# A planned instruction order for the second attention: other starting times, two early slab loads, 196 shifted ranks, and another order of the last down sweeps

## The chip, the cores and the metric

The kernel runs on one core of one Trainium2 chip. The metric is the device time of one execution in microseconds (us), as the median of several runs. The parts of the core that matter here are TensorE (PE, with its weight loads PEld), VectorE (DVE), ScalarE (ACT), GpSimd (POOL) and SyncE (SP), which issues the DMAs. Each engine works through its own instructions in the order in which they were issued to it; an instruction that waits holds up all that stands behind it on its engine.

## The reference, cut to what matters

Two layers over 1024 latent tokens and 256 context tokens, with 1024 features in fp32. Layer 0 mixes with a neighbourhood attention, layer 1 with a sliding-window attention; each layer ends with a gated feed-forward.

```python
for i in range(DEPTH):                                   # DEPTH = 2
    h  = modulate(rmsnorm(x, g_attn[i]), sh1, sc1)       # shift, scale, gate from SiLU(c)
    hc = modulate(rmsnorm(ctx, g_attn[i]), sh1c, sc1c)
    q, k, v = attn_inputs(h, w_in, gq, gk, n_kv)         # one projection, RMS norm of q and k per head
    ...                                                  # layer 1: rotary, then banded softmax with a
    o = sliding_window_attention(q, k, v, k_c, v_c, sink)  # sink logit, 16 heads in 4 key groups
    x = x + gt1 * (o @ w_out)
    h = modulate(rmsnorm(x, g_ffn[i]), sh2, sc2)
    x = x + gt2 * conv_ffn(h, w_up[i], conv_w[i], conv_b[i], w_down[i])
```

## The kernel before, in words

Every fp32 product is done as three matmuls on a high and a low part of each operand (`whi`, `wlo` of a weight; `h1hi`, `h1lo` or `n1lo` of the activations). Splitting a weight takes a DMA into a `raw` buffer (three of them), a copy on ACT (`whi`) and a subtraction on DVE or POOL (`wlo`).

The kernel is a row of stages: layer 0's attention, its feed-forward `ffn(0)`, layer 1's attention (here: the second attention), and `ffn(1)`. In each stage the work is written as operations with an engine, a planned duration, what they read and write, and a key. A planner (`Sched`) plays the stage through: at each moment every free engine takes the ready operation with the smallest key, if the buffers that it needs are free in the plan. The instructions are then issued in the order that came out, and that order is fixed. `Sched.rank` adds a number from a table (`RANKS`) to the keys of some operations, named by their index. The stage of the first attention has such a table (`na`), and both feed-forwards have one; the second attention has none.

`Sched.run(free)` takes the times at which the engines become free; the second attention calls it without, so that in the plan all engines are free at time 0, though on the chip the queues still hold the end of `ffn(0)`.

The second attention goes like this. `plan_ctx_kv` projects the context to keys and values (`mm<-whi,h1chi`, weights `ckv`), which have their own norm (`ckvv`, `ckvy`) and end in the tile `ckc`. `plan_norm` normalises the second half of the tokens: it needs the sums of squares (`sums`), loads that half back from DRAM (`x<-x_dram`, four tiles), and makes `t`, `h1hi` and `n1lo` from it. The first half is ready when the stage begins (`h1hi`, `h1lo`). For each of 4 key groups, four `slab` tiles of weights are loaded and split, eight token tiles are projected (`plan_sw_qkv`: `mm`, then `qraw`, `qsq`, `qv`, a power on POOL `qy`, the rotary `qa` and `qb`, and transposes `pt<-idr,st`), and sixteen units of softmax follow (`plan_sw_su`: scores `s`, maximum on DVE, a copy of the sink logit on POOL `S<-sink`, exponential on ACT `S<-S,m`, transposes `pt<-idr,S`, their split `pthi`, `ptlo`, and the products `pv`). The last group's units are mixed with the output projection of the first 512 tokens (`mm<-o0hi,whi`), for which stored heads are loaded back (`oraw`) with the reciprocals of their sums, multiplied and split (`o0hi`, `o0lo`, and `o1hi`, `o1lo` for the second 512).

The feed-forward ends with five sweeps over the down weights (`plan_pair`, matmuls `dn`), numbered 0 to 4. Sweep 2 fills the four banks `c`, whose results each go to one output tile; sweep 4 fills the four banks `d`, each of which goes to two. `plan_ev` adds a bank to its output tile on DVE (`xn<-dn,modc,xn`), `plan_xd` stores the tile.

Of the kernel before, what the change touches and what calls it, by code (L numbers as in the profile page):

```python
# [11 lines left out]
F32 = mybir.dt.float32  # L12
F32R = mybir.dt.float32r
AF = mybir.ActivationFunctionType
# [3 lines left out]
P = 128  # L18
# [20 lines left out]
class InOrder:  # L39
# [7 lines left out]
    def __getattr__(self, name):  # L47
        f = getattr(self.eng, name)

        def call(*a, **k):  # L50
# [31 lines left out]
          19.7},  # L82
    ffn1={286: 3.3, 290: 17.8, 2323: -3.8},
)


class Sched:
# [6 lines left out]
                                       pool=(0.15, 0.08, 0.06, 0.1), dma=(0.0, 0.0, 0.0, 0.0)).items()  # L94
# [164 lines left out]
def trunk_kernel(ctx, tc, xperm, xtok, xseq, cc, wmod0, wmod, bmod, gnorm, na_wqkv, na_gq, na_gk, na_bias, na_wo,  # L259
# [38 lines left out]
    dve.memset(invd, 1.0 / D)  # L298
    dsh = spool.tile([P, 112], F32, name="dsh")[:, :8]
    mhalf = cpool.tile([P, 16], F32, name="mhalf")  # L300
# [67 lines left out]
    def t_dve(n):  # L368
        return 0.065 + n / 960.0

    def t_act(n):
        return 0.094 + n / 1200.0
# [4 lines left out]
    def t_pool(n):  # L377
        return 0.15 + n / 480.0
# [59 lines left out]
    class Slabs:  # L438
# [29 lines left out]

        def plan(self, sc, i, key, uses):
            sc.op("dma", 1.4, lambda e: self.load(i), writes=[("raw", i)], key=key - 7, acq=[("raw", ("raw", i), 2)])  # L470
            sc.op("act", t_act(768), lambda e: self.hi(i), reads=[("raw", i)], writes=[("wh", i)], key=key - 2,
                  acq=[("w", ("w", i), uses)], rel=[("raw", i)])
            sc.op(*self.engs, lambda e: self.lo(i, e), reads=[("raw", i), ("wh", i)],
                  writes=[("wl", i)], key=key - 2, rel=[("raw", i)])

# [192 lines left out]
    def plan_norm(sc, l, psa, wk, sums, x, hl, key):  # L668
# [68 lines left out]
        for k in range(KT):  # L737
            hi = hl[0][:, k, :]

            def mul(e, k=k):  # L740
                B["t", k] = wk.tile([P, 512], F32, tag=("pthi", "ptlo")[k % 2], name="t", bufs=PTB)
                dve.scalar_tensor_tensor(out=B["t", k][:, :n], in0=x[:, k, :], scalar=modc[:, l, 0, 1, k:k + 1], in1=B[f[1]][:, :n],
                                         op0=ALU.mult, op1=ALU.mult)
            sc.op("dve", t_dve(n) + 0.06 * l, mul, reads=[f, ("x1", k)], writes=[K("t", k)], key=key, rel=[f],
                  acq=[(("pthi", "ptlo")[k % 2], K("t", k), 1)], port=l == 0)
# [21 lines left out]
            for k, lof in los[-2:]:  # L767
                sc.op(*(("pool", t_pool(n)) if l == 1 and k % 2 else ("dve", t_dve(n))), lof, reads=[K("hi", k), K("t", k // 2 * 2 + 1)], writes=[(f"h{l}", 1, k)], key=key, rel=[K("t", k)])

# [308 lines left out]
    NWAIT = (2, 3, 4)  # L1078
    NREADY = 8.0
    NPRE = 3  # L1080
# [277 lines left out]
    def ffn(l, opj, xt1, todo):  # L1358
# [694 lines left out]
        def plan_pair(si, i):  # L2053
# [60 lines left out]
            for q in range(nq):  # L2114
                d, starts = prods[q]
                for m in range(4):
                    def mm(e, q=q, m=m, d=d, starts=starts):
# [6 lines left out]
                    sc.op("pe", 3 * t5, mm, reads=[I + (t, q) for t in ("gh", "gl", "wh", "wl")] + u_done,  # L2124
                          writes=[("dn", d, m)], key=k0 + 2.72 * q + (1.36 * m - 2.72 * (i - NP + 2) if si == 4 and i >= NP - 2 else 0),
                          acq=[("b", ("d" + d, m), dict(a=3, b=2, c=1, d=2)[d])] if starts and i == 0 else (),
# [10 lines left out]
        def plan_xd(c, k, key):  # L2137
# [6 lines left out]
            sc.op("dma", 0.9, out_, reads=[("xn", c, k)], writes=[("xd", c, k)], key=key, rel=[("xnt", c, k // 2)])  # L2144
        for si in range(5):
            for i in range(NP):
                plan_pair(si, i)
            ke = KS[si + 1]
            if si == 0:
# [47 lines left out]
    def plan_next(sc, KS, xn, bank, x_tile, plan_sums, plan_bc, plan_t, plan_hilo, u_done, gp, D_):  # L2197
# [85 lines left out]
        for i in range(4):  # L2283
# [10 lines left out]
            def lo(e, i=i):  # L2294
# [9 lines left out]
    slabs = Slabs(sw_wqkv, WL1)  # L2304
    ffn(0, op0, None, [0, 1])
    gqk, sink, bandt, rc, rs = [C1[n] for n in ("gqk", "sink", "bandt", "rc", "rs")]
# [345 lines left out]
    h[1] = [hpool.tile([P, KT, 512], F32R, tag="hhi", name="h1hi", bufs=2), Parts([None] * 4, 2)]  # L2652
    sc.hold("raw", "sums1", 1)
    for i in range(4):
        sc.hold("w", ("cw", i), 2)
    for tag in ("s", "pt"):
        psa(tag, F32)
    plan_ctx_kv()
    for j in range(0, KT, 2):
        sc.op("dma", 1.2, lambda e, j=j: dma.dma_start(  # L2660
            xs[1].tiles[j // 2], x_dram[:, (KT + j) * 512:(KT + j + 2) * 512].rearrange("p (k t) -> p k t", k=2)),
            writes=[("x1", j), ("x1", j + 1)], key=-206)
# [50 lines left out]
    xt1 = plan_oproj1()  # L2713
    sc.run()
    ph.close()
# [118 lines left out]
```

## Time and profile before

| | us |
|---|---|
| median of 3 runs | 2786.18 |
| lowest, highest | 2782.22, 2786.51 |
| the profiled execution | 2783.58 |
| its span in the profile | 2781.8 |
| PE busy in the span | 2750.7 (99%) |
| DVE, ACT, POOL busy | 2260.3, 1693.5, 409.8 |

The span is the time from the first to the last instruction of the profiled execution. In the timeline of the profile a row gives its start, its duration, its engine, the operation with its output and inputs, and in brackets how long the engine had stood idle before it and what ended that wait. All operations pass through one helper, so that every row has the line L51; operations are told apart by the names of their tiles.

### The profile page before, as it was taken

How to read it: one execution, taken by the hardware profiler on the slowest of the kernel's cores; microseconds unless marked ns; L12 is line 12 of the kernel's file. 1: busy time of each engine (PE TensorE's matmuls, PEld its weight loads, DVE VectorE, ACT ScalarE, POOL GpSimd, SP SyncE). 2: the span in 40 equal slices, each digit the busy share in tenths (PEclk: the TensorE clock that was granted, in tenths of full speed). 3: DMA queues.
4: the chain of work that ended last, by engine and by line, in shares of the span. 5: the costliest groups of instructions: out<-in, count | busy, mean ns of one | idle time of the engine just before them, and what ended most of it. 6: DMA issues, size and time to landing. Idle time of an engine off the chain costs nothing.

```text
span 2781.8 us, 45781 instructions
## 1 busy us (share of the span) xinstructions
PE 2750.7 (99%) x16297; PEld 2439.2 (88%) x16297; DVE 2260.3 (81%) x4982; ACT 1693.5 (61%) x3320; POOL 409.8 (15%) x662
## 2 busy tenths in 40 slices
PE   8999999999999999999999999999999999999999
PEld 7999999999899987777788879999988888888887
DVE  6887888888789687877788688888886988888757
ACT  6776776788556544445454457888863655455443
POOL 1222222223100000000000007545430000000000
PEclk9999999999999999999999999999999999999999
DMA  7222222224745543444466561000255322324745
GB/s 284 81 83 91 71 73 73 90 80 132 253 152 189 184 163 133 163 148 144 152 222 235 170 223 39 24 24 20 72 187 179 104 107 98 114 105 144 256 151 189
DMA packets 144870, 375.63 MB, mean 135 GB/s; under 512 B 22144, under 2 KB 35072, under 8 KB 143232
## 3 DMA queue, kind: packets, MB, share of 16 engines
q1 hardware_dynamic: 144640, 372.70, 39.8%
q8 instruction: 128, 2.10, 0.3%
q14 instruction: 102, 0.84, 0.1%
HBM read 305.59 MB, written 67.04 MB: 134 GB/s over the span
## 4 chain that ended last, share of the span: by engine, by line
PE 95%; DVE 2%; DMA 1%; ACT 1%; issue 0%; POOL 0%; SPq 0%; DVEq 0%; ACTq 0%
PE mm L51 18%; PE ua L51 17%; PE dn L51 15%; PE uc L51 13%; PE pt L51 7%; PE pv L51 6%; PE s L51 5%; PE oacc L51 5%; PE ud L51 4%; PE dnc L51 2%; PE u L51 2%; PE mod L51 1%; DMA x<-in_xperm_dram 0%; DMA slab<-in_sw_wqkv_dram 0%; DVE S L51 0%
## 5 line engine op out<-in xcount | busy, mean ns | idle before, releaser
L51 ACT ACTIVATE whi<-wraw 128x512 fp32r<-128x512 f32 (+1 forms) x264 | 213.1, 808 | 200.5 <-PE uc L51 58.4
L51 DVE TENSOR_TENSOR wlo<-wraw,whi 128x512 fp32r<-128x512 f32 (+1 forms) x264 | 240.2, 911 | 41.4 <-ACT whi L51 41.0
L51 DVE TENSOR_TENSOR ptlo<-pt,pthi 128x512 fp32r<-128x512 f32 (+2 forms) x384 | 223.9, 596 | 34.9 <-ACT pthi L51 31.7
L51 ACT ACTIVATE S<-S,m 128x640 f32<-128x640 f32 (+3 forms) x288 | 221.0, 769 | 38.0 <-DVE m L51 29.6
L51 PE MATMUL dn<-ghi,whi 128*128 128x512 f32 x616 | 239.8, 389 | 0.0
L51 PE MATMUL dn<-ghi,wlo 128*128 128x512 f32 x616 | 239.7, 389 | 0.0
L51 PE MATMUL dn<-glo,whi 128*128 128x512 f32 x616 | 239.6, 389 | 0.0
L51 ACT ACTIVATE pthi<-pt 128x512 fp32r<-128x512 f32 (+2 forms) x384 | 196.3, 524 | 64.1 <-PE pt L51 48.8
L51 DVE SCALAR_TENSOR_TENSOR u<-c,cv,u 128x1023 f32<-128x1023 f32 x176 | 222.9, 1279 | 6.4 <-ACT u L51 5.4
L51 ACT ACTIVATE whi<-s 128x1024 fp32r<-128x1024 f32 (+1 forms) x116 | 109.0, 939 | 181.8 <-PE uc L51 129.3
L51 ACT ACTIVATE ghi<-graw 128x512 fp32r<-128x512 f32 x154 | 96.3, 630 | 177.5 <-PE dn L51 102.2
L51 PE MATMUL pt<-idr,S 128*128 128x128 f32 x1280 | 196.5, 274 | 3.2 <-DVE qt L51 2.2
L51 PE MATMUL mm<-whi,h0hi 128*128 128x384 f32 x480 | 172.2, 359 | 0.6 <-ACT qraw L51 0.6
L51 DVE TENSOR_TENSOR glo<-graw,ghi 128x512 fp32r<-128x512 f32 x154 | 105.3, 688 | 73.0 <-ACT ghi L51 67.1
L51 PE MATMUL mm<-wlo,h0hi 128*128 128x384 f32 x480 | 162.3, 338 | 0.0
L51 PEld LDWEIGHTS pt<-idr,S 128*128 128x128 f32 x1280 | 150.4, 141 | 10.7 <-ACT kkl L51 2.3
L51 DVE TENSOR_TENSOR wlo<-s,whi 128x1024 fp32r<-128x1024 f32 (+1 forms) x116 | 124.7, 1075 | 39.2 <-ACT whi L51 39.1
L51 POOL TENSOR_TENSOR qy<-qv,mhalf 128x4 f32<-128x4 f32 (+1 forms) x112 | 121.5, 1088 | 156.4 <-DVE qv L51 134.9
L51 POOL TENSOR_TENSOR n1y<-n1v,mhalf 128x4 f32<-128x4 f32 (+1 forms) x8 | 8.2, 1026 | 922.5 <-DVE n1v L51 922.5
L51 PEld LDWEIGHTS dn<-glo,whi 128*128 128x128 f32 x616 | 115.6, 188 | 24.1
L51 PEld LDWEIGHTS dn<-ghi,whi 128*128 128x128 f32 x616 | 115.6, 188 | 24.1
L51 PEld LDWEIGHTS dn<-ghi,wlo 128*128 128x128 f32 x616 | 115.6, 188 | 23.7
(386 smaller groups left out, 8828.0 us busy)
## 6 DMA issues: line engine op xcount, KB each, us to landing
wraw<-in_w_up_dram SPq DMA_DIRECT2D x132, 512.0 KB, 3.5
wm<-in_wmod_dram SPq DMA_DIRECT2D x80, 512.0 KB, 3.9
wraw<-in_w_down_dram SPq DMA_DIRECT2D x44, 512.0 KB, 4.1
graw<-g_dram SPq DMA_DIRECT2D x44, 512.0 KB, 4.4
wraw<-in_w_down_dram SPq DMA_DIRECT2D x88, 256.0 KB, 3.1
graw<-g_dram SPq DMA_DIRECT2D x66, 256.0 KB, 2.8
slab<-in_na_wqkv_dram SPq DMA_DIRECT2D x32, 384.0 KB, 3.9
woraw<-in_na_wo_dram SPq DMA_DIRECT2D x24, 512.0 KB, 4.2
```

Of the source, the lines that this page charges most:

```text
L51: r = f(*a, **k)
```

## The change

The second attention is planned with other numbers:

- its planner starts with ACT, DVE, POOL and SP busy for 5.5, 9.0, 0.5 and 9.0 us (`LAG`);
- operations without an instruction (`stored`) hold back the loads of the four `x` tiles in the plan until given times; the norm's tiles `n1lo` now wait in the plan for the release of the `x` tiles (`xl`); a `raw` buffer may be released out of order;
- a small ACT operation (`table`, on one column) stands early in the stage, so that the table of the exponential is loaded there;
- the loads of the first two `slab` tiles are issued by `plan_next`, at the end of `ffn(0)`, and the splits of the first group's slabs get a key of their own;
- 196 operations get a shift of their key (`RANKS["sw"]`); the norm's key goes from -260 to 5, and `NREADY` from 8.0 to 9.2 (a planned time of the first attention).

In `ffn(1)` the sweeps run in the order 0, 1, 3, 4, 2 in place of 0, 1, 2, 3, 4 (`ffn(0)` keeps its order).

```diff
+    sw={7: 5.7, 60: 47.4, 133: -7.4, 167: -41.6, 188: 22.2, 198: -62.9, 214: 25.5, 231: 15.5, 238: 3.4, 256: 1.9,
...
-    ffn1={286: 3.3, 290: 17.8, 2323: -3.8},
+    ffn1={286: 3.3, 290: 17.8, 2330: -3.8},
...
+    LAG = dict(act=5.5, dve=9.0, pool=0.5, dma=9.0)
+    STORED = {0: 2.0, 2: 7.5, 4: 3.0, 6: 10.0}
+
+    def table(sc, f, src, tok, key):
+
+        sc.op("act", 1.4, lambda e: act.activation(small[:, 64:65], src(), f, scale=0.0), reads=[tok], writes=[("table",)], key=key)
...
-    NREADY = 8.0
+    NREADY = 9.2
...
-        KS = [KD, KD + 60, KD + 120, KD + 150, KD + 180, KD + 210]
+        SWEEPS = (0, 1, 3, 4, 2) if last else (0, 1, 2, 3, 4)
+        KS = {si: KD + (0, 60, 120, 150, 180)[q] for q, si in enumerate(SWEEPS)}
...
+        for i in range(NSLAB):
+            sc.op("dma", 1.4, lambda e, i=i: slabs.load(i), reads=[("slr", 3), ("sll", i)], writes=[("slab", i)], key=KS[5] - 30,
+                  acq=[("raw", ("slab", i), 1)])
...
-    sc = Sched(dict(CAPS, qraw=3))
+    sc = Sched(dict(CAPS, qraw=3, xl=4), {"raw"})
...
     plan_ctx_kv()
+    table(sc, AF.Exp, lambda: CK["v", 0][:, 0, :1].bitcast(F32), ("ckv", "vh", 0), 5.0)
     for j in range(0, KT, 2):
+        sc.op(f"stored{j}", STORED[j], lambda e: None, writes=[("stored", j)], key=-300)
...
-    plan_norm(sc, 1, psa, wk, sums1, xs[1], h[1], -260)
+    plan_norm(sc, 1, psa, wk, sums1, xs[1], h[1],  5)
...
-            slabs.plan(sc, 4 * g + j, 16 * g + QKEY1 if g else -200, 8)
+            slabs.plan(sc, 4 * g + j, 16 * g + QKEY1 if g else -200, 8, None if g else -262)
...
-    sc.run()
+    sc.rank(RANKS["sw"])
+    sc.run(LAG)
```

What this does to the order is shown at three places. Where names end in a number, it is the number of the tile.

**Start, SP and DVE.** The last stores of `ffn(0)` (`x_dram<-xn`), the slab loads, and the four `x` tiles of the norm. SP before:

```order
L51 DMA ckv<-in_sw_ckv_dram 128x1024
L51 DMA x_dram<-xn 128x512 x4
L51 DMA slab<-in_sw_wqkv_dram 128x768 x2
L51 DMA x_19655<-x_dram 128x1024
L51 DMA x_19656<-x_dram 128x1024
L51 DMA x_19657<-x_dram 128x1024
L51 DMA x_19658<-x_dram 128x1024
L51 DMA slab<-in_sw_wqkv_dram 128x768 x9
```

SP in the changed kernel:

```order
L51 DMA ckv<-in_sw_ckv_dram 128x1024
L51 DMA x_dram<-xn 128x512 x3
L51 DMA slab<-in_sw_wqkv_dram 128x768
L51 DMA x_dram<-xn 128x512
L51 DMA slab<-in_sw_wqkv_dram 128x768 x3
L51 DMA x_19659<-x_dram 128x1024
L51 DMA x_19660<-x_dram 128x1024
L51 DMA x_19661<-x_dram 128x1024
L51 DMA x_19662<-x_dram 128x1024
L51 DMA slab<-in_sw_wqkv_dram 128x768 x7
```

The first slab moves ahead of one store, and the third and fourth slabs ahead of the four `x` tiles. On DVE in the same place, where `S` is the diagonal matrix of the norm's factors, `t` the normed second half and `wlo` the low part of a slab, before:

```order
L51 TENSOR_SCALAR S<-idr,n1y 128x128 x4
L51 TENSOR_REDUCE ckvv<-qsq 128x4
L51 TENSOR_TENSOR vc<-S,vc 128x4x64
L51 TENSOR_TENSOR wlo<-slab,whi 128x768
L51 SCALAR_TENSOR_TENSOR t<-x_19655,modc,s 128x512 x2
L51 SCALAR_TENSOR_TENSOR t<-x_19656,modc,s 128x512 x2
```

and in the changed kernel:

```order
L51 TENSOR_SCALAR S<-idr,n1y 128x128 x4
L51 TENSOR_TENSOR wlo<-slab,whi 128x768
L51 TENSOR_REDUCE ckvv<-qsq 128x4
L51 TENSOR_SCALAR ckvv<-ckvv 128x8
L51 SCALAR_TENSOR_TENSOR t<-x_19659,modc,s 128x512 x2
L51 SCALAR_TENSOR_TENSOR t<-x_19660,modc,s 128x512
L51 TENSOR_TENSOR wlo<-slab,whi 128x768
```

Three `t` operations, and so the loads of the first two `x` tiles, now stand ahead of the low part of the fourth slab (before, POOL made that one; now POOL makes the first slab's, ahead of the norm's power). On PE, six more matmuls stand ahead of `pt<-invd,sums` and twelve `mm` in place of six ahead of `s<-S,ones`.

**The table, ACT.** The first rows of ACT after the split of the second slab, before (the load of the table stands 50 rows further down, ahead of the first `S,rs<-S,m`):

```order
L51 ACTIVATE S<-mm 128x512
L51 ACTIVATE qsq<-S 128x256
L51 ACTIVATE vc<-S 128x4x64
L51 ACTIVATE S<-mm 128x512
L51 ACTIVATE whi<-slab 128x768
```

and in the changed kernel:

```order
L51 ACTIVATE S<-mm 128x512
L51 ACTIVATE qsq<-S 128x256
L51 ACTIVATE vc<-S 128x4x64
L51 ACT_TABLE_LOAD
L51 ACTIVATE dsh<-vc 128x1
L51 ACTIVATE whi<-slab 128x768
L51 ACTIVATE S<-mm 128x512
```

The load of the table and its one-column operation stand ahead of the third slab's `whi` and of the second evacuation `S<-mm`.

**End of the stage, POOL.** The last units of softmax and the first stored heads of the second 512 tokens (`oraw`, `o1lo`). Before:

```order
L51 TENSOR_TENSOR st<-qa,st 128x4x64
L51 COPY S<-sink 128x1 x2
L51 TENSOR_TENSOR osb<-osb,rb 128x512
L51 COPY S<-sink 128x1
L51 TENSOR_TENSOR oraw<-oraw 128x512
L51 COPY S<-sink 128x1
L51 TENSOR_TENSOR oraw<-oraw 128x512
L51 TENSOR_TENSOR o1lo<-oraw,o1hi 128x512 x2
L51 COPY S<-sink 128x1 x3
```

and in the changed kernel:

```order
L51 COPY S<-sink 128x1
L51 TENSOR_TENSOR klt<-qa,st 128x128
L51 COPY S<-sink 128x1
L51 TENSOR_TENSOR st<-qa,st 128x4x64
L51 TENSOR_TENSOR oraw<-oraw 128x512 x2
L51 TENSOR_TENSOR o1lo<-oraw,o1hi 128x512 x2
L51 COPY S<-sink 128x1
L51 TENSOR_TENSOR oraw<-oraw 128x512
L51 COPY S<-sink 128x1 x2
```

No copy of a sink stands between the first two `oraw` any more; the next copy follows both and two `o1lo`. On PE, 33 rows of output projection that stood behind the last `pv` of the stage now stand among the last units.

More of the change, by code (lines that the diff above doesn't have):

```diff
@@ L298, in trunk_kernel @@
     dve.memset(invd, 1.0 / D)
-    dsh = spool.tile([P, 112], F32, name="dsh")[:, :8]
+    small = spool.tile([P, 112], F32, name="dsh")
+    dsh = small[:, :8]
     mhalf = cpool.tile([P, 16], F32, name="mhalf")
@@ L467, in ahead, with plan @@
                 self.lo(i, "pool" if i % 2 else "dve")
-        def plan(self, sc, i, key, uses):
-            sc.op("dma", 1.4, lambda e: self.load(i), writes=[("raw", i)], key=key - 7, acq=[("raw", ("raw", i), 2)])
-            sc.op("act", t_act(768), lambda e: self.hi(i), reads=[("raw", i)], writes=[("wh", i)], key=key - 2,
+        def plan(self, sc, i, key, uses, kw=None):
+            kw = key - 2 if kw is None else kw
+            if i not in self.raw:
+                sc.op("dma", 1.4, lambda e: self.load(i), writes=[("raw", i)], key=key - 7, acq=[("raw", ("raw", i), 2)])
+            sc.op("act", t_act(768), lambda e: self.hi(i), reads=[("raw", i)], writes=[("wh", i)], key=kw,
                   acq=[("w", ("w", i), uses)], rel=[("raw", i)])
             sc.op(*self.engs, lambda e: self.lo(i, e), reads=[("raw", i), ("wh", i)],
-                  writes=[("wl", i)], key=key - 2, rel=[("raw", i)])
+                  writes=[("wl", i)], key=kw, rel=[("raw", i)])
     def plan_qkv_mm(sc, key, psa, h, tt, slabs, s, J, c0=0, hkey=None):
@@ L2144, in plan_xd @@
             sc.op("dma", 0.9, out_, reads=[("xn", c, k)], writes=[("xd", c, k)], key=key, rel=[("xnt", c, k // 2)])
-        for si in range(5):
+        for si in SWEEPS:
             for i in range(NP):
                 plan_pair(si, i)
-            ke = KS[si + 1]
+            ke = KE[si]
             if si == 0:
@@ L2653, in trunk_kernel @@
     sc.hold("raw", "sums1", 1)
+    for i in range(NSLAB):
+        sc.hold("raw", ("raw", i), 2)
     for i in range(4):
```

12 lines of the change are left out of this document (8 added, 4 removed), and 21 rows, old and new, of the table sw.

## The prediction

> **What bounds the kernel now.** I read the head of the profile's page first, then PE's busy time by stretches, then the timeline at the ends of PE's waits. The stretches are in this order: start and end in us, length, busy us and instructions of PE, PEld, DVE, ACT and POOL, the granted clock of PE, the DMA share, GB/s. The last row is of PE alone.
>
> ```profile
> span 2781.8 us, 45781 instructions
> ```
>
> ```profile
> 390.00:700.00 310.00, 309.52 (x2303) 300.98 (x2302) 264.66 (x942) 242.39 (x614) 83.37 (x97) 1.00 0.31 94
> 1648.00:1680.00 32.00, 29.09 (x151) 25.30 (x150) 24.77 (x47) 21.50 (x40) 10.45 (x10) 1.00 0.65 226
> 1680.00:1740.00 60.00, 58.08 (x399) 55.96 (x399) 50.21 (x164) 44.19 (x113) 46.10 (x79) 1.00 0.11 32
> 1800.00:1860.00 60.00, 58.86 (x437) 57.35 (x436) 53.81 (x167) 51.44 (x132) 32.17 (x69) 1.00 0.14 39
> 1860.00:2000.00 140.00, 140.00 (x1044) 138.08 (x1043) 121.92 (x406) 118.30 (x298) 67.96 (x149) 1.00 0.12 34
> 2000.00:2045.00 45.00, 40.15 (x250) 33.92 (x249) 41.93 (x111) 34.65 (x78) 20.44 (x39) 0.96 0.45 147
> ```
>
> ```profile
> 2040.00:2043.40 3.40, 3.40 (x16) 0.50 0.38 127
> ```
>
> PE is the bound. In the second attention (about 1650 to 2068) it idles 2.91 us in the first stretch, 1.92 in the second, 1.14 around 1800 and 4.85 at the end; between 1860 and 2000 it does not stop. Its clock is at half speed for 3.40 us, which loses 1.7. So the stage has 10.8 us of idle time and 1.7 us of clock: 12.5 us is all that another order can win there, because the same products are computed. What an order with few waits reaches is seen in the first attention, whose ranks are tabled already: 0.48 us idle in 310.
>
> The profiled execution took 2783.58, 1.8 more than its span; the median shown is 2786.18, 2.6 more than that. I make the sum against 2783.58 and add 2.6. What a measurement can tell from no change is taken as 0.2%, 5.6 us.
>
> **Part A, the start: lag, early slabs, x tiles.** The timeline's rows, and from the view of a tile the times from issue to landing of `x` and of `slab`:
>
> ```profile
> 1651.73 0.39 PE L51 MATMUL mm<-wlo,h1chi 128*128 128x512 f32 x1
> ...
> 1652.98 4.04 SPq L51 DMA_DIRECT2D slab<-in_sw_wqkv_dram  x2
> ...
> 1656.49 0.39 PE L51 MATMUL mm<-wlo,h1chi 128*128 128x512 f32 x1
> 1656.58 1.41 DVE L51 TENSOR_TENSOR sums<-sums,sq 128x512 f32<-128x512 f32 x2
> ...
> 1657.07 1.87 SPq L51 DMA_DIRECT2D x<-x_dram  x4
> ...
> 1657.18 0.84 ACT L51 ACTIVATE whi<-slab 128x768 fp32r<-128x768 f32 x1 [2.36 <-DMA slab<-in_sw_wqkv_dram]
> ...
> 1658.04 1.05 PE L51 MATMUL pt<-invd,sums 128*128 128x1 f32 x8 [0.49 <-DVE sums L51]
> ...
> 1663.64 1.16 PE L51 MATMUL s<-S,ones 128*128 128x128 f32 x8 [0.60 <-DVE S L51]
> ...
> 1666.92 0.84 ACT L51 ACTIVATE whi<-slab 128x768 fp32r<-128x768 f32 x1 [4.30 <-DMA slab<-in_sw_wqkv_dram]
> ...
> 1667.81 0.45 PE L51 MATMUL mm<-whi,h1hi 128*128 128x384 f32 x1 [1.42 <-ACT whi L51]
> ...
> 1668.67 2.71 DVE L51 SCALAR_TENSOR_TENSOR t<-x,modc,s 128x512 f32<-128x512 f32 x4
> ...
> 1669.31 1.84 POOL L51 TENSOR_TENSOR wlo<-slab,whi 128x768 fp32r<-128x768 f32 x1
> ```
>
> ```profile
> DMA to landing us min/median/max: 3.9/6.2/7.4
> ```
>
> ```profile
> DMA to landing us min/median/max: 2.9/3.6/7.9
> ```
>
> The two `mm` rows are the first and the last of 22 of one size in a row: 4.76 / 21 = 0.227 us for each. The wait of 0.49 for `sums` is covered by the six matmuls that now stand before it (6 x 0.227 = 1.36), the wait of 0.60 for `S` by twelve in place of six. The wait of 1.42 is for the third slab, which landed near 1666.9 because it was issued behind the four `x` tiles. Now it is issued ahead of them, once the first slab's split frees its `raw` buffer: that slab's `whi` at 1657.18, 0.7 sooner, with 0.84 for itself and 1.84 for POOL's `wlo`, gives 1659.2. With the median of 3.6 it is there at 1662.8, four us sooner. All three go, and what comes next is late instead: the `x` tiles. They were issued at 1657.07; now the third slab (1659.2) and the fourth, 2.0 later at the rate of the first two (4.04 for two), go ahead of them, and with 1.87 / 4 = 0.47 for that issue itself they go out near 1661.7, 4.6 later. Three `t` need the first two of them and stand on DVE ahead of the fourth slab's `wlo`, so 0.3 to 0.9 us of new wait are likely. Of 2.91 I count 2.0 as won. Bounds: 2.91 if the loads land early, -1.5 if the first slab's `wlo`, which moves to POOL beside DVE's `sums` (a POOL split of a slab takes 1.84), holds up `sums` for its whole length.
>
> [...]
>
> **Part B, the table, and part C, POOL beside DVE.** From the timeline, the middle of the stage:
>
> ```profile
> 1702.01 1.28 ACT L51 ACT_TABLE_LOAD   x1
> ...
> 1705.21 1.15 PE L51 MATMUL pt<-idr,S 128*128 128x128 f32 x8 [0.32 <-ACT kll L51]
> ...
> 1708.45 0.44 PE L51 MATMUL mm<-whi,h1hi 128*128 128x384 f32 x1 [0.36 <-ACT qraw L51]
> ...
> 1719.80 0.28 PE L51 MATMUL pt<-idr,st 128*128 128x128 f32 x1 [0.96 <-DVE ptlo L51]
> ```
>
> ```profile
> 1799.82 1.85 POOL L51 TENSOR_TENSOR wlo<-slab,whi 128x768 fp32r<-128x768 f32 x1
> 1799.85 1.85 DVE L51 SCALAR_TENSOR_TENSOR qy<-qt,qy 128x5 f32<-128x5 f32 x1
> ...
> 1802.85 0.25 PE L51 MATMUL pt<-idr,st 128*128 128x128 f32 x1 [1.10 <-DVE ptlo L51]
> ```
>
> The table's load of 1.28 us stood at 1702 on ACT, ahead of the first exponential, and PE's waits of 0.32 and 0.36 on ACT follow it. In the changed kernel it stands before the third slab's `whi`, where ACT had stood idle for 4.30: it costs there 0 to 0.3, counted in part A. The 0.68 go. Of the other 1.24 of this stretch (0.96 is one wait for `ptlo`) half, as the shifts move operations that PE waits for. B is 1.3, between 0 and 1.92.
>
> At 1799.85 a DVE operation on 5 elements took 1.85, exactly as long as POOL's split of a slab beside it; PE then waits 1.10. These POOL splits stay, only their neighbours change, so I count half: C is 0.6, between -1.1 (one more such meeting) and 1.14.
>
> **Part D, the end.** From the timeline:
>
> ```profile
> 2026.86 1.21 DVE L51 TENSOR_TENSOR wlo<-woraw,whi 128x1024 fp32r<-128x1024 f32 x1
> ...
> 2034.44 1.30 POOL L51 TENSOR_TENSOR oraw<-oraw 128x512 f32<-128x512 f32 x1 [4.17 <-DMA oraw<-r_dram]
> 2034.48 2.34 DVE L51 TENSOR_TENSOR wlo<-woraw,whi 128x1024 fp32r<-128x1024 f32 x1
> ...
> 2035.67 1.19 POOL L51 COPY S<-sink 128x1 f32<-128x1 f32 x1
> ...
> 2036.90 0.83 ACT L51 ACTIVATE S<-S,m 128x641 f32<-128x641 f32 x1 [2.63 <-POOL S L51]
> ...
> 2038.98 0.47 PE L51 MATMUL pv<-pthi,vc 128*128 128x256 f32 x2 [2.45 <-ACT pthi L51]
> ...
> 2039.51 1.29 POOL L51 TENSOR_TENSOR o1lo<-oraw,o1hi 128x512 fp32r<-128x512 f32 x1 [1.43 <-ACT o1hi L51]
> ```
>
> POOL waits 4.17 for a transfer to multiply `oraw`; the one-element sink copy stands behind it and takes 1.19, since DVE's `wlo` holds it up (that one takes 2.34 instead of 1.21); ACT's exponential waits 2.63 for the copy, PE 2.45 for what follows, and a us later the clock is at 0.50. In the changed order 12, 9 and 6 matmuls of output projection stand between the last units on PE where 6, 9 and 9 stood, so the critical wait has 6 x 0.227 = 1.36 us more to do: 2.45 - 1.36 = 1.09, and a little less if the copy isn't held; I take 0.8 as what is left, 1.65 as won. A wait of 0.8 should not drop the clock, since the longest one at the start, 1.42, is followed by a clock of 1.00: 1.7 won. Of the other 2.40 us of idle time here half: 1.2. D is 4.55, between 0 and 6.55.
>
> [...]
>
> **Part E, the sweeps.** From the timeline, the last bank's additions with their issue times taken together, and the last matmul:
>
> ```profile
> 2773.36 5.49 DVE L51 SCALAR_TENSOR_TENSOR xn<-dn,modc,xn 128x512 f32<-128x512 f32 x8 [2.67 <-PE dn L51]
> ...
> 2777.01 0.39 PE L51 MATMUL dn<-ghi,wlo 128*128 128x512 f32 x1
> ```
>
> Each addition takes 5.49 / 8 = 0.69, and the last ends at 2778.85, 1.45 behind the last matmul (2777.40): two for the last bank. With sweep 2 at the end each bank has one, which ends near 2777.40 + 0.69 = 2778.1: 0.75 won, between 0 and 0.75. The eight additions and stores of sweep 4 now stand inside, with the matmuls of a whole sweep behind them as cover.
>
> **Part F, new waits.** The loads of `x` are 4.6 later, and the second half's low parts follow from them:
>
> ```profile
> 1679.84 1.29 POOL L51 TENSOR_TENSOR n1lo<-t,h1hi 128x512 fp32r<-128x512 f32 x1
> ...
> 1683.11 0.33 PE L51 MATMUL mm<-whi,n1lo 128*128 128x384 f32 x1
> ```
>
> The last `n1lo` ended at 1681.13, 2 us before PE needed the first, and the last is needed some 3 us after the first (an estimate): about 5 us of cover for 4.6 of delay. I take -0.5, between 0 and -4.
>
> **Sum.** 2.0 + 1.3 + 0.6 + 4.55 + 0.75 - 0.5 = 8.7. The profiled execution comes to 2783.58 - 8.7 = 2774.9, the median to 2777.5. The most that all bounds give is 13.3: 2772.9.
>
> **Rivals.** *All waits go*, as in the first attention's row with its 0.48 in 310: the stage's 400 us would keep about 0.6, so 12.5 - 0.6 + 0.75 = 12.7 are won, 2773.5. For it: every wait found has work ahead of it in the new order. Against it: `x` is later.
>
> *The x tiles become the bound*: if they land at the upper end (7.4 from 1661.7: 1669.1), then three `t` (2.71 / 4 = 0.68 each) and a `wlo` (0.69 x 768 / 512 = 1.04, by the size of part E's additions) put the fourth slab's low part at about 1672.2. PE, without its waits of 0.49, 0.60 and 1.42, begins the third slab at 1667.81 - 2.51 = 1665.3 and has 24 matmuls of 384 columns, 24 x 0.227 x 384 / 512 = 4.1, before it wants the fourth, at 1669.4: 2.8 idle. With part F at -1.2 (0.7 more) and 0.5 of that wait counted in part A already, the sum falls by 2.8 + 0.7 - 0.5 = 3.0: 5.7 won, 2780.5.
>
> *The waits only move*, or the change does not do what it says: the first slab goes out a mere 0.7 sooner (one store sooner), POOL's splits meet other DVE operations, and half of the end's gap stays. A, B, C give 0.5 together, D 2.2, E 0.75: 3.4 won, 2782.8.
>
> *Slower: the sink copy stands behind the heads on POOL.* In the new order no copy stands between the first two `oraw`, and the next one follows both and two `o1lo`. If the loads of the heads land late again, the copy is behind 4.17 of waiting and 2 x 1.30 + 2 x 1.29 = 5.18 of work, and PE has only 12 x 0.227 = 2.72 of other work: 6.6 idle and 1.7 of clock, 8.3 in all, and a second time at the next pair: 16.7 in place of today's 2.45 + 1.7. With the other parts (2.0 + 1.3 + 0.6 + 1.2 + 0.75 - 0.5 = 5.35 won) the change would cost 16.7 - 4.15 - 5.35 = 7.2: 2793.4. It decides when the heads land more than the filler, 2.7 us, after the copy is wanted. Against it: the order has the copies of the units before moved ahead of the first `oraw`.
>
> **How the numbers follow.** The forecast (6 to 12 won) gets 0.40, all waits gone 0.25, late `x` tiles 0.14, waits that only move 0.11, the slower case 0.10. Under 2780.6 (faster by over 0.2%) lie the forecast and the second case; the third stands at the border, and the forecast's own edge gives the rest of it away: 0.65. Within 0.2%: 0.25. Slower: 0.10. The range reaches from the most that can be won, 2772.9, less the 3.7 by which the lowest run shown lies under the median, to the waits that only move with 2 us for their bounds: 2769.2 to 2785.0; it leaves out the slower case and the edges.
>
> **What would show it.** Right, if in the changed kernel the first stretch has under 1 us of idle PE, no wait of 2 us or a clock of 0.50 appears between 2030 and 2045, and the last addition ends within 0.8 of the last matmul. Part A is wrong if PE waits for the fourth slab's `wlo` or DVE's `sums` takes twice its time; part F if a wait for `n1lo` appears near 1680; part D if ACT waits over 2 us for `S<-sink`, which with a lower clock behind it makes the whole forecast wrong.

## The result and the profile after

The changed kernel takes 2777.17 us (median of 13 runs, 2775.31 to 2778.43); the kernel before, in 13 runs, 2783.60 (2780.76 to 2786.51). The ratio is 0.9978, 95% interval 0.9969 to 0.9986: faster by 6.4 us, between 0.14% and 0.31%. The profiled execution is the one of 2777.17.

The head of the page and PE's stretches, of the changed kernel (columns as before):

```profile
span 2775.4 us, 45798 instructions
PE 2747.6 (99%) x16297; PEld 2436.5 (88%) x16297; DVE 2254.4 (81%) x4987; ACT 1691.1 (61%) x3321; POOL 412.2 (15%) x657
...
1648.00:1680.00 32.00, 29.29 (x157) 25.40 (x156) 25.99 (x55) 22.08 (x40) 8.54 (x7) 1.00 0.68 230
1680.00:1740.00 60.00, 57.94 (x401) 56.25 (x400) 48.64 (x154) 45.15 (x118) 46.74 (x79) 1.00 0.11 32
1800.00:1860.00 60.00, 59.66 (x441) 58.12 (x440) 53.23 (x175) 51.33 (x130) 32.79 (x68) 1.00 0.14 39
2000.00:2045.00 45.00, 43.03 (x268) 36.45 (x268) 39.93 (x110) 36.21 (x81) 23.59 (x35) 1.00 0.51 169
```

The start idles 2.71 us where it idled 2.91, the second stretch 2.06 for 1.92: nothing was won there. The stretch around 1800 went from 1.14 to 0.34, the end from 4.85 to 1.97, and the clock stays at 1.00. What PE waited for from 1640 to 2070 (total, times, longest; four of nine lines):

```profile
PE pt L51 <- DVE ptlo L51: 2.0, 2, 1.4
PE mm L51 <- DVE wlo L51: 1.5, 1, 1.5
PE pt L51 <- ACT kll L51: 1.3, 2, 1.0
PE mm L51 <- POOL n1lo L51: 0.6, 1, 0.6
```

New among them are the fourth slab's `wlo`, a `ptlo` near 1713, a `kll` near 2036, and `n1lo`. The timeline of the changed kernel around the first two, with POOL's split of the first slab ahead of them:

```profile
1657.11 0.85 ACT L51 ACTIVATE whi<-slab 128x768 fp32r<-128x768 f32 x1 [1.56 <-DMA slab<-in_sw_wqkv_dram]
...
1658.09 2.32 POOL L51 TENSOR_TENSOR wlo<-slab,whi 128x768 fp32r<-128x768 f32 x1 [8.96 <-ACT whi L51]
...
1662.87 1.89 SPq L51 DMA_DIRECT2D x<-x_dram  x4
...
1668.75 2.06 DVE L51 SCALAR_TENSOR_TENSOR t<-x,modc,s 128x512 f32<-128x512 f32 x3 [2.20 <-DMA x<-x_dram]
...
1671.74 0.45 PE L51 MATMUL mm<-wlo,h1hi 128*128 128x384 f32 x1 [1.47 <-DVE wlo L51]
...
1709.64 1.84 POOL L51 TENSOR_TENSOR wlo<-slab,whi 128x768 fp32r<-128x768 f32 x1 [0.24 <-ACT whi L51]
...
1709.66 2.23 DVE L51 TENSOR_TENSOR qa<-qn,rc 128x256 f32<-128x256 f32 x2
...
1713.45 0.63 PE L51 MATMUL pt<-idr,S 128*128 128x128 f32 x4 [1.42 <-DVE ptlo L51]
```

DVE stands idle for 2.20 until the `x` tiles land, with the fourth slab's low part behind three `t`. And two `qa` take 2.23 beside POOL's split of a slab. From the view of the tile `x`, its times from issue to landing:

```profile
DMA to landing us min/median/max: 5.8/7.0/8.5
```

`Sched.run` counts 2.0 us for that behind the issue. Three of the kernels below keep this order of SP and DVE up to here (one `qa` move near 1710, that move and a `qt`, the table in its old place). In their profiles the first of these tiles landed 3.9, 4.1 and 4.6 us behind its issue instead of 5.8, and PE's wait for the fourth slab's `wlo` was 1.61, 0.48 and 0.48 instead of 1.47. So the size of that wait is one execution's.

To compare kernels without what lies ahead of the stage (its start differs by up to 2.9 us between these profiles), I use three lengths read from the rows' starts: from the stage's first matmul to the last `oacc` of its output projection, from there to the last matmul, and from that one's end to the end of the span. "Waits" is the sum of PE's idle times over 0.1 us in the first part; "half clock" says whether a stretch near 0.50 lies in it. Each row is one profiled execution; where that one lies more than 1 us off the median of its kernel's runs, the text says so.

| kernel | stage | waits in it | half clock | to the last matmul | tail |
|---|---|---|---|---|---|
| before | 486.65 | 10.7 | at 2040 | 641.12 | 4.40 |
| before, profiled again | 486.42 | 10.0 | near 1670 | 641.12 | 4.41 |
| changed | 480.22 | 7.1 | no | 641.17 | 3.65 |

### The profile page after: what moved, and what is told of

Its sections match the earlier page's. It is cut to its first block, busy times and chain, and to the rows that moved or that the text cites. A ratio compares the mean times of both kernels' runs of the same rounds, so it can differ in the third digit from the quotient of the medians.

```text
span 2775.4 us, 45798 instructions
## 1 busy us (share of the span) xinstructions
PE 2747.6 (99%) x16297; PEld 2436.5 (88%) x16297; DVE 2254.4 (81%) x4987; ACT 1691.1 (61%) x3321; POOL 412.2 (15%) x657
## 4 chain that ended last, share of the span: by engine, by line
PE 94%; DMA 2%; DVE 1%; ACT 1%; POOL 1%; issue 1%; SPq 0%; POOLq 0%; DVEq 0%; ACTq 0%
PE mm L51 18%; PE ua L51 17%; PE dn L51 15%; PE uc L51 13%; PE pt L51 7%; PE pv L51 6%; PE s L51 5%; PE oacc L51 5%; PE ud L51 4%; PE dnc L51 2%; PE u L51 2%; PE mod L51 1%; DMA oraw<-r_dram 1%; DMA x<-in_xperm_dram 0%; DMA wm<-in_wmod_dram 0%
```

## The experiments

All are the one or the other kernel with one or a few operations moved in the order that the planner put out, if nothing else is said. The move is made just before the operations are issued; a number is an operation's index, and the comment says what it is.

```diff
+        for i, where, j in getattr(self, "moves", ()):
+            order.remove(i)
+            order.insert(order.index(j) + (where == "after"), i)
         for i in order:
             ops[i]["fn"](on[i])
```

**The ranks alone.** The changed kernel without one line:

```diff
-    sc.rank(RANKS["sw"])
     sc.run(LAG)
```

> The changed kernel without its 196 shifted ranks; the lag, the early slabs, the held-back x tiles, the table and the sweeps stay. Theory: the ranks are what takes away the waits in the middle and at the end of the stage (parts B, C and D), so that the stage from its first matmul to the end of the output projection is 3 to 6 us longer than the 480.2 of the changed kernel, with PE waits behind `S<-sink` or `ptlo` at the end again; 2780 to 2783 in all. Rival: the lag and the early slabs carry the gain, since with them the plan agrees with the chip's queues; the stage stays within 1 us of 480.2.

Measured: 2783.40, ratio to before 1.0000 (0.9991 to 1.0009), stage 487.40 with 10.8 us of waits. PE's waits in it, two stretches (of PE alone), and rows of the timeline:

```profile
PE pt L51 <- DVE ptlo L51: 3.4, 4, 2.5
PE pv L51 <- DVE osb L51: 3.2, 4, 1.2
PE mm L51 <- POOL n1lo L51: 1.7, 1, 1.7
...
1648.00:1680.00 32.00, 31.24 (x175) 1.00 0.64 214
2000.00:2045.00 45.00, 38.16 (x251) 1.00 0.51 160
...
1663.92 1.82 DVE L51 TENSOR_TENSOR wlo<-slab,whi 128x768 fp32r<-128x768 f32 x2
1665.99 0.75 DVE L51 SCALAR_TENSOR_TENSOR t<-x,modc,s 128x512 f32<-128x512 f32 x1
...
1690.82 0.45 PE L51 MATMUL mm<-whi,n1lo 128*128 128x384 f32 x1 [1.69 <-POOL n1lo L51]
```

The theory holds for the sum: with the ranks taken out of this plan the stage is as long as before (1.7 of the 487.40 are a stretch at half clock, with 0.57 granted from 1692 to 1696, as before has one). By place it is not so simple. Up to 1680 PE idles 0.76 here, where before has 2.91 and the changed kernel 2.71: lag, early slabs and held-back tiles win 2.1 there without any rank, and it is the ranks that put three `t` ahead of the fourth slab's low part (here both low parts stand ahead of the `t`). What is won there is lost again behind it: 1.7 for `n1lo`, and from 2000 to 2045 PE idles 6.84 where before has 4.85. The ranks without the lag and the early slabs were not run, so what either part is worth beside the other is not shown.

**The sweeps alone**, on the kernel before: the order 0, 1, 3, 4, 2 with the keys that go with it.

```diff
-        KS = [KD, KD + 60, KD + 120, KD + 150, KD + 180, KD + 210]
+        SWEEPS = (0, 1, 3, 4, 2) if last else (0, 1, 2, 3, 4)
...
```

> The kernel before, with the order of the last down sweeps changed to 0, 1, 3, 4, 2 and nothing else. Theory (part E): the last addition ends 0.7 instead of 1.45 us behind the end of the last matmul, 0.75 us won, no new PE wait between 2500 and 2777. Rival: the eight additions and stores of sweep 4, now inside, hold up the next sweep: PE waits there by 0.5 us or more, and nothing is won.

Measured: tail 3.66 in place of 4.40, to the last matmul 641.13 in place of 641.12. The last matmul and the last addition in its timeline:

```profile
2774.43 0.39 PE L51 MATMUL dn<-ghi,wlo 128*128 128x512 f32 x1
2774.85 0.75 DVE L51 SCALAR_TENSOR_TENSOR xn<-dn,modc,xn 128x512 f32<-128x512 f32 x1 [0.61 <-PE dn L51]
```

One addition ends 0.78 behind the last matmul's end, and nothing waits inside. The whole time (2781.17, ratio 0.9997, 0.9988 to 1.0006) can't show 0.7 us by itself. But the tail is 3.65 to 3.67 in every profile of a kernel with the new sweeps, eleven in all with the changed kernel's, and 4.40 to 4.41 in the three with the old ones.

**The sink copy**, on the kernel before: the first `oraw` goes behind the last copy.

```diff
+    sc.moves = [(2934, 'after', 2775)]   # POOL: oraw (1, 0) behind S<-sink
```

> The kernel before, with one move: on POOL the last sink copy at the end of the second attention (the one that took 1.19 us) stands ahead of the first `oraw` of the second 512 tokens instead of behind it. Theory (part D of the prediction): PE's wait of 2.45 us and the stretch at half clock behind it both hang on that copy. Then PE's idle time between 2034 and 2045 falls below 0.6 us, no granted clock of 0.50 appears there, and the time falls by 2.45 + 1.7 = 4.1 us, about 0.15%. Rival: another wait is right behind (the exponential's DVE inputs, or `o1hi` on ACT), PE still waits 1.5 us or more and the clock falls all the same: 0 to 1 us won.

Measured: 2781.76, ratio 0.9997 (0.9989 to 1.0006); the profiled execution, 2783.61, is the slowest of the 11. PE's first wait for `pv` there is 0.29, and the end keeps its clock, but the half clock is elsewhere (stretches of PE: granted clock behind the busy time):

```profile
1668.30 0.44 PE L51 MATMUL mm<-whi,h1hi 128*128 128x384 f32 x1 [1.76 <-ACT whi L51]
...
1668.00:1675.00 7.00, 6.32 (x26) 0.76 0.38 121
2036.00:2045.00 9.00, 8.35 (x53) 1.00 0.49 139
...
2035.96 1.29 POOL L51 TENSOR_TENSOR oraw<-oraw 128x512 f32<-128x512 f32 x1 [2.69 <-DMA oraw<-o_dram]
```

The stage is 486.75, as long as before: PE's waits come to 10.0 instead of 10.7, as 0.6 more of them stand at the start and smaller ones at the end, the half clock is lost as before, and 0.8 more passes outside of waits. The copy no longer stands behind the heads, and the wait of 2.45 is gone. But POOL also waited only 2.69 for the heads instead of 4.17, and the next run has a wait of 0.61 with the copy in its old place; how much of the 2.45 the copy itself is worth is not shown. The 4.1 us that the theory expected lie outside the interval of the time (3.1 us at most).

**Before, once more.** The kernel before, unchanged, for a second profile (a comment at its head makes the line L52).

> The kernel before, once more with a profile. Theory: the same waits of PE stand at the same places (2.4 at the end, 1.1 near 1802), but whether a wait is followed by a stretch at a granted clock of 0.50 differs from execution to execution, and the part of the time from the first matmul of the stage to the end of the output projection is 485 without such a stretch and 486.7 with one. Rival: the clock falls behind the 2.4 us at the end in every execution, as in the first profile.

```profile
1667.82 0.44 PE L52 MATMUL mm<-whi,h1hi 128*128 128x384 f32 x1 [1.79 <-ACT whi L52]
...
2034.70 1.29 POOL L52 TENSOR_TENSOR oraw<-oraw 128x512 f32<-128x512 f32 x1 [2.08 <-DMA oraw<-r_dram]
...
2038.70 0.48 PE L52 MATMUL pv<-pthi,vc 128*128 128x256 f32 x2 [0.61 <-ACT pthi L52]
...
1668.00:1675.00 7.00, 6.63 (x29) 0.76 0.39 115
2040.00:2043.40 3.40, 3.40 (x26) 1.00 0.61 184
```

Measured: 2783.98, ratio 1.0000 (0.9990 to 1.0010), stage 486.42 (from an execution 1.2 us under the median). It is the same program, and POOL waits 2.08 for the load instead of 4.17, PE 0.61 instead of 2.45; the clock falls behind the 1.79 at the start and not at the end. By the trace's rows for SP, the load of the heads landed 5.1 us behind its first issue instead of 6.1, which is half of the 2.1 that POOL waits less; for the other half POOL itself came to it 1.1 later behind that issue. With the kernel of the sweeps alone, which has the same order up to there, it is the other way about: a wait of 2.40 with no fall at all, and a stage of 485.42.

```profile
2037.50 0.48 PE L51 MATMUL pv<-pthi,vc 128*128 128x256 f32 x2 [2.40 <-ACT pthi L51]
...
2037.50:2044.00 6.50, 6.50 (x42) 1.00 0.53 177
```

So the theory was right on the clock and wrong on the waits: the 2.4 at the end isn't in every execution either, since it depends on when the heads land and on when POOL and PE come to them. Of the four profiles with this order of the stage (the two of before, the sweeps, the copy) three have a stretch at half clock, at two different places. In the second attention of all profiles here, waits of PE of 1.69 (without ranks), 1.76, 1.79, 1.90 (five moves, below) and 2.45 us were followed by half clock, waits of 1.82 (the last version below), 2.40 and 2.48 (without ranks) were not, and none up to 1.61 was.

**The fourth slab's low part**, on the changed kernel:

```diff
+    sc.moves = [(87, 'before', 54)]   # DVE: wlo of slab 3 ahead of the first t
```

> The changed kernel, with one move on DVE: the low part of the fourth slab stands ahead of the three `t` that wait for the late `x` tiles. Theory: PE's wait of 1.47 us for that `wlo` is due to this order alone; it goes, and 1.0 to 1.5 us are won against the changed kernel (about 2776.0 where that has 2777.2), with a wait for `n1lo` of up to 0.6 us left. Rival: the slab's own data are late as well (transfer, `whi`), the wait stays above 0.8 us and under 0.5 us is won; or the second half is then late by as much, and a new wait for `n1lo` above 1 us takes the gain back.

**The x tiles first**, on the changed kernel:

```diff
+    sc.moves = [(40, 'before', 85), (42, 'before', 85)]   # SP: two x tiles ahead of slab 3
```

> The changed kernel, with one move on SP: the first two `x` tiles are issued ahead of the fourth slab, whose issue waited for a free buffer in any case. Theory: the `x` tiles go out about 2 us sooner, the three `t` start 1.5 to 2 us sooner, and PE's wait of 1.47 us for the fourth slab's `wlo` falls below 0.4; 1.0 to 1.8 us won. Rival: the transfers of `x` wait for something else (they land when the slabs' transfers are through), `t` starts less than 0.5 us sooner and the wait stays; no change within 0.5 us.

Measured: 2775.86 (ratio to before 0.9976, 0.9967 to 0.9986) and 2775.15 (0.9972, 0.9962 to 0.9982); the stages are 478.74 and 478.90, 1.5 and 1.3 shorter than the changed kernel's. Both profiled executions lie 1.1 to 1.3 us under the median of their runs, and the intervals of the ratios overlap with the changed kernel's, so the whole time does not show the gain. The rows of the first, then of the second:

```profile
1665.62 0.99 DVE L51 TENSOR_TENSOR wlo<-slab,whi 128x768 fp32r<-128x768 f32 x1
1666.53 1.39 DVE L51 SCALAR_TENSOR_TENSOR t<-x,modc,s 128x512 f32<-128x512 f32 x2
...
1671.26 0.44 PE L51 MATMUL mm<-whi,h1hi 128*128 128x384 f32 x1 [0.27 <-ACT qraw L51]
```

```profile
1659.06 0.90 SPq L51 DMA_DIRECT2D x<-x_dram  x2
...
1664.79 2.06 DVE L51 SCALAR_TENSOR_TENSOR t<-x,modc,s 128x512 f32<-128x512 f32 x3
```

In both PE no longer waits for that `wlo`. In the second the tiles go out 2.1 us sooner with respect to the stage's start (10.85 instead of 12.91 behind it) and DVE has no idle time left ahead of `t`. Either order takes that wait away; the late `x` and the place of the `t` are one cause. What it is worth is less sure than 1.5 and 1.3, as the same wait was 0.48 in two other executions of the changed order.

**The table** in its old place: the early one-column operation keeps its place in the plan, but issues nothing.

```diff
-    sc.op("act", 1.4, lambda e: act.activation(small[:, 64:65], src(), f, scale=0.0), ...
+    sc.op("act", 1.4, lambda e: None, ...
```

> The changed kernel in its order, but the one-column ACT operation that stands early in the stage has no instruction, so that the exponential's table is loaded at the first exponential (near 1701) again. Theory (part B): PE waits on ACT for 0.3 to 0.4 at two places behind the load, 0.7 us lost against the changed kernel; the early load itself cost nothing there. Rival 1: the load is covered at both places, no change within 0.3 us. Rival 2: the early load holds up the third slab's `whi`, and without it the start is 0.5 us or more shorter.

```profile
1704.20 1.28 ACT L51 ACT_TABLE_LOAD   x1
...
1707.07 0.98 PE L51 MATMUL pt<-idr,S 128*128 128x128 f32 x7 [0.38 <-ACT S L51]
```

Measured: 2777.30, stage 480.94 (from an execution 1.4 us above the median). A wait of 0.38 for the exponential's `S` is back, and the stage is 0.7 longer, as the theory says; but the wait of 1.42 near 1713 is gone, since the two `qa` now came ahead of POOL's split (0.55 from 1710.69, the split at 1711.02), and others near 2050 came. The time agrees with no change too, so this stays open.

**DVE beside POOL near 1710.** On the changed kernel, first the `qa` moved, then a `qt` besides:

```diff
+    sc.moves = [(200, 'after', 372)]                      # DVE: qa behind ptlo
+    sc.moves = [(200, 'after', 372), (226, 'after', 395)] # and qt behind the ptlo that follows
```

> The changed kernel, with one move on DVE near 1710: the two `qa` (2.23 us in the changed kernel, beside POOL's split of a slab) stand behind the `ptlo` that PE waits 1.42 us for, instead of ahead of it and of two operations on `s`. Theory: PE's wait is due to these two `qa` being held up beside POOL's `wlo` of the slab; it falls below 0.3 us and 1.1 to 1.4 us are won. Rival: `ptlo` itself is held up in the same way, or `pthi` on ACT is as late, and the wait stays above 1 us.

The timeline with the first move:

```profile
1709.45 0.55 DVE L51 TENSOR_TENSOR qa<-qn,rc 128x256 f32<-128x256 f32 x2
...
1711.23 1.84 POOL L51 TENSOR_TENSOR wlo<-slab,whi 128x768 fp32r<-128x768 f32 x1
1711.39 1.70 DVE L51 SCALAR_TENSOR_TENSOR qt<-qt,qv 128x5 f32<-128x5 f32 x1
...
1714.67 0.44 PE L51 MATMUL pt<-idr,S 128*128 128x128 f32 x2 [1.04 <-DVE ptlo L51]
```

The two `qa` take 0.55 now instead of 2.23, and the old wait is gone; but POOL's next split catches a five-element `qt`, and PE waits 1.04. Stage 480.63: nothing won (2776.69, ratio 0.9975, 0.9966 to 0.9984).

> The changed kernel with the `qa` move near 1710, and a second one: the five-element `qt`, which took 1.70 us beside POOL's next split of a slab once `qa` was out of the way, stands behind the following `ptlo`. Theory: what costs PE 1.42 us there is whichever DVE operation with two inputs in SBUF stands beside POOL's splits; with both out of their way no PE wait above 0.3 us is left between 1700 and 1720, and the stage is 1.0 to 1.4 us shorter than with the first move alone. Rival: the next such operation (`klt`, `osb`) is caught instead, a wait near 1 us stays.

With both moves no wait is left between 1700 and 1720, and the stage is 477.32 (2776.38, ratio 0.9971, 0.9960 to 0.9982). But the profiled execution, 2773.31, is the fastest of seven and 3.1 us under their median, so the 477.32 is not this kernel's usual stage. Of its 3.3 us against the first move 1.0 are the wait that is gone. 1.1 are a wait for the fourth slab's `wlo`, 0.48 in this profile and 1.61 in the other, and 1.3 waits at the end that this execution did not have; 0.6 more of small waits at the start and 0.5 less outside of waits nearly cancel. In the profile of the first move the second `x` tile landed 0.4 later, and the `wlo` met a POOL operation:

```profile
1668.58 1.27 POOL L51 TENSOR_TENSOR n1lo<-t,h1hi 128x512 fp32r<-128x512 f32 x1 [1.48 <-ACT h1hi L51]
...
1668.95 1.73 DVE L51 TENSOR_TENSOR wlo<-slab,whi 128x768 fp32r<-128x768 f32 x1
```

That `wlo` takes 0.95 in the profile with both moves. Near 1710, too, the operation that begins first keeps its time: the split its 1.84, and the two `qa` that begin 0.02 behind it grow from 0.55 to 2.23. Not every DVE operation grows there: beside the changed kernel's next split, at 1713.11, `S<-s` took 0.60 and `ptlo` 0.67, as elsewhere, and both read a bank that matmuls fill.

**Moves together.** Five moves (the two `x` tiles count as one; 2938 is one `o1hi` on ACT, which goes behind `kkl` and `kll`):

```diff
+    sc.moves = [(87, 'before', 54), (40, 'before', 85), (42, 'before', 85), (200, 'after', 372),
+                (2938, 'after', 2457), (77, 'before', 139)]   # 2938: o1hi on ACT; 77: the last n1lo ahead of one qb
```

> The changed kernel with five moves: the fourth slab's low part ahead of the three `t` on DVE, two `x` tiles ahead of the fourth slab on SP, the `qa` near 1710 behind `ptlo`, the last `n1lo` ahead of one `qb` on POOL, and one `o1hi` near 2035 behind the two copies `kkl` and `kll` on ACT. Theory: each wait has its own cause, so the gains add: 1.5 + 1.4 + 0.6 + 0.9 = 4.4 us less, stage 476 us, 2772.8 in all. Rival: the later waits take up what the earlier ones give, and no more than 2 us are won (2775).

```profile
1672.98 0.44 PE L51 MATMUL mm<-whi,h1hi 128*128 128x384 f32 x1 [1.90 <-ACT qraw L51]
...
1673.40:1676.80 3.40, 3.40 (x15) 0.50 0.00 0
```

The rival holds: 2778.02, stage 480.50 (from an execution 1.5 us under the median). 1.7 of the stage are the half clock behind the wait of 1.90; without it the stage would be 478.8, no better than with either cure of the start alone, though it has three more moves. The two cures together make a wait longer than the one that either took away, as the fourth slab now lands late (its `whi` begins 3.5 behind the third's, 1.7 in the changed kernel) and all `t` stand behind its low part (the first begins at 1668.5). Then without that move, with `qt`, and with one `oraw` moved on DVE:

```diff
+    sc.moves = [(40, 'before', 85), (42, 'before', 85), (200, 'after', 372), (226, 'after', 395),
+                (77, 'before', 139), (2938, 'after', 2457), (2949, 'after', 2782)]   # 2949: oraw on DVE
```

> The changed kernel with the moves that have not got in each other's way: two `x` tiles ahead of the fourth slab on SP (without the move of that slab's low part), `qa` and `qt` near 1710 behind the `ptlo`, the last `n1lo` ahead of one `qb`, `o1hi` near 2035 behind `kkl` and `kll`, and one `oraw` near 2042 on DVE, which waits for its load, behind the `ptlo` that PE needs. Theory: 1.3 + 1.4 + 0.6 + 0.9 + 0.6 = 4.8 us less, the stage near 475.5, 2772.5 in all. Rival: two or more of the waits come back at the next operation; not under 2774.5.

Measured: 2773.55 (2772.92 to 2775.58), ratio to before 0.9962 (0.9948 to 0.9976), stage 478.47: between the theory and its rival, with waits of 0.84 near 1672 (for `qraw`) and 1.21 near 2044. And the same without 2938 and 2949:

> The changed kernel with the moves at the start and in the middle only: two `x` tiles ahead of the fourth slab, `qa` and `qt` near 1710 behind the `ptlo`, the last `n1lo` ahead of one `qb`; the end of the stage is left as the changed kernel has it. Theory: the moves that act through DVE beside POOL and through the issue of `x` are worth 1.3 + 1.4 + 0.6 us at places that do not move from execution to execution, so PE's idle time up to 1800 falls from 4.7 us to under 2 and the stage to 477 or less. Rival: as in the version with five moves, a new wait for `whi` or `qraw` near 1672 of 0.8 us or more takes a part back; the stage stays above 477.5.

Measured: 2774.03 (2772.80 to 2775.04), ratio 0.9963 (0.9949 to 0.9976), stage 478.64 (from an execution 1.0 us above the median): PE's waits up to 1800 come to 1.3 instead of 4.6, as the theory says, but the stage does not reach 477. A wait of 0.73 for `qraw` stands near 1672, and the one behind an `oraw` on DVE at the end, 0.62 in the changed kernel, is 1.8 here:

```profile
2040.13 0.69 DVE L51 TENSOR_TENSOR oraw<-oraw 128x512 f32<-128x512 f32 x1 [2.56 <-DMA oraw<-r_dram]
```

Both versions are faster than the changed kernel by 3 to 4 us by the medians of five runs each, of which the stages of their profiles show 1.6 to 1.8; the intervals of the ratios still overlap with its own.

## Why the prediction was right, and where it was not

The forecast of 2777.5 is met within 0.3 us by luck, with two errors that cancel: the gain against the profiled execution was put at 8.7 and is 6.4, and the 2.6 that were added for the median of three runs are not there, as the median of 13 is 2783.60. By the gain alone the rival of the late `x` tiles, with 5.7, came closer. Of the three signs for being right, the last addition (0.8 behind the last matmul) and the end without a wait of 2 us or a clock of 0.50 are met; the first stretch, with 2.71 us of idle PE instead of under 1, is not, and the sign against part A, a wait for the fourth slab's `wlo`, is there. The bounds of the range have a slip: the lowest run shown lies 3.96 under the median, not 3.7, and the upper one is 2782.8 + 2 = 2784.8, not 2785.0; the result is far from both.

**A (2.0 won): wrong.** The waits went from 2.88 (0.49, 0.60, 1.42, 0.37) to 2.66 (0.24, 1.47, 0.41, 0.54), 0.2 won. The named step that failed is "0.3 to 0.9 us of new wait" for the `x` tiles; it was 1.47, the mechanism of the rival on `x` and not of the forecast. The tiles went out 0.4 later in the stage than reckoned (12.91 behind its start, not 1661.7 - 1649.23 = 12.47), since POOL's split of the first slab took 2.32 and not 1.84, and `t` began 5.9 after that. The prediction's own rows, with the median landing of 6.2, gave 1661.7 + 6.2 + 2.04 + 1.04 - 1669.4 = 1.6; it took 0.3 to 0.9 without that sum. Its size is chance in part: in two of the four profiles with this order the wait is 0.48, inside 0.3 to 0.9, and in two 1.47 and 1.61. The rival's own 2.8 was not reached in any. The waits of 0.41 and 0.54 behind it were not foreseen. The bound of POOL's split beside `sums` did not come: `pt<-invd,sums` has no wait, and it was the split that got longer. The early load brought the first `whi` forward by 0.8 (7.15 instead of 7.95 behind the stage's start), as reckoned.

**B (1.3 won): wrong.** The listed waits are all gone, and a new one of 1.42 stands near 1713: 0.45 won. The step that failed is counting POOL's meetings with DVE for C alone: a new order can make one in B's stretch as well, and the trace of the first move near 1710 shows that the delay goes on to the next operation in line (a `qt` of five elements, 1.70). That the early table is what took away the 0.68 is not shown: without it one wait of 0.38 for the exponential is back, but the time does not tell.

**C (0.6): 0.8 won. E (0.75): 0.75 won. F (-0.5):** the wait for `n1lo` is 0.58.

**D (4.55): right for this pair of profiles,** wrong as a mean. Idle time fell by 2.9 (0.3 of it came back behind 2045) and the clock gave 1.7: 4.3. But the second profile of the kernel before has a wait of 0.61 there, without a fall of its clock. The step that failed is reading the 2.45 and its 1.7 as fixed: what can be counted on is less, for the clock about 1.3 if three of four profiles of the old order stand for all (an estimate). That this chance makes the wider spread of the kernel before (5.75 us between its 13 runs, 3.1 for the changed kernel) is not shown.

**What the sum left out.** That 12.5 us was all another order could win isn't so. Without waits and clock the stage of before takes 486.65 - 10.7 - 1.7 = 474.3, that of the changed kernel 480.22 - 7.1 = 473.1, 1.1 less with the same matmuls; the other three profiles of the old order give 474.7 to 475.0 in the same way, so the difference is 1.1 to 1.9. From one matmul to the next the output tile's name changes 755 times before, 725 after; that this is what the 1.1 comes from is not shown (without ranks there are 750 and 474.9, with a stretch of half clock taken off at 1.7).

Together: 0.2 + 0.45 + 0.8 + 4.3 + 0.75 - 0.6 + 1.1 = 7.0, less the 0.7 by which this execution came later to the stage: 6.3 of the 6.4.

**The rivals.** All waits gone: no, 7.1 us are left. The late `x` tiles: the mechanism came, at half its size or less. The waits that only move: this is what A and B did, 0.65 won together where 3.3 were forecast; C, D and E did not. The slower case did not come, though the order is as told: the copy behind both `oraw` and both `o1lo` had been put where the exponential wants it later (ACT does not wait for it), and PE's waits there are 0.96 (for `kll`, behind `o1hi`) and 0.62. The heads landed early as well, so the case that was priced was not put to the test:

```profile
2031.88 3.54 POOL L51 TENSOR_TENSOR oraw<-oraw 128x512 f32<-128x512 f32 x2 [1.33 <-DMA oraw<-r_dram]
```

What part A takes for granted, that the lag and the early loads are worth something by themselves, is so at the start of the stage (2.1 in the run without ranks) and not for the stage as a whole.

## What to carry to other kernels

Where a planner sets the order, the waits that are left sit where its costs are furthest from the chip: here a load planned to land 2.0 us behind its issue that takes 3.9 to 8.5 in four profiles, and two engines that hold each other up (two `qa` behind the start of POOL's split took 2.23, and 0.55 out of its way). Repair such a wait only with the operation behind it in view, since another took its place in two of these runs (`qa` alone, and the five moves). Before a wait of one profile is counted as a gain, profile the same kernel a second time, and look where the profiled execution lies among the runs: a wait for a transfer, and the clock behind it, may be that execution's own, as the 2.45 with its half clock, which was 0.61 without it the second time.

## What the runs showed of the hardware

The same program had a PE wait of 2.45 us at one place in one execution and of 0.61 in another, in part by the landing of one load (6.1 and 5.1 us behind its issue; POOL waited 4.17 and 2.08 for it). A load of one `x` tile, in the same place of the order, landed 3.9 to 5.8 us behind its issue in four profiles. Without the ranks, a wait of 1.69 us was followed by half clock and one of 2.48 was not. A five-element DVE operation that began behind a POOL subtraction of 128x768 took 1.70 where such an operation takes 0.16 elsewhere; it came into that place when the two `qa` that had taken 2.23 were moved out of the way.
